# Shared keys of two heads in seven block products, and adaLN products moved and partly kept in float32

## The chip, the cores and the metric

The kernel runs on one core of a Trainium2 chip. The metric is the device time of one execution in microseconds (us); of several runs the median is taken. The core has TensorE (PE in the profile; its weight loads are PEld), VectorE (DVE), ScalarE (ACT), GpSimd (POOL) and SyncE (SP), which here only issues transfers.

## The reference

One step of a streaming encoder with two layers. 640 rows run through it: 512 of a prompt, and 8 sequences of 16 new rows. Layer 0 is a gated linear recurrence, layer 1 is stick-breaking attention over one shared set of keys and values. Width 2048, 16 heads of 128, all in float32.

```python
def ada_mod(c, w, b):
    m = jax.nn.silu(c) @ w + b          # c: 9 rows; w: 2048 x 6144
    shift, scale, gate = jnp.split(m, 3, axis=-1)
...
def shared_kv(x, g_kv, w_kv):
    k, v = jnp.split(rms_norm(x, g_kv) @ w_kv, 2, axis=-1)
...
for l in range(DEPTH):
    shift, scale, gate = ada_mod(c, w_ada[l], b_ada[l])
    hn = rms_norm(x, g_pre[l]) * (1.0 + scale) + shift
    # layer 0: out = recurrent_mixer(hn, ...)
    # layer 1: k_new, v_new = shared_kv(x, g_kv, w_kv); out = stick_breaking_mixer(hn, ...)
    x = x + gate * rms_norm(out, g_post[l])
```

The keys are 640 x 2048 by 2048 x 2048, and so are the values. adaLN has 9 rows of conditioning, so its products are thin.

## The kernel before

**Split products.** Float32 precision comes from two parts. A matrix is split into a high part, rounded by ScalarE (line 87), and a low part, the difference, made by VectorE (line 88). A product is then three on TensorE (lines 101 to 103): high by high, high by low, low by high. Weights arrive in raw tiles by SP's queue, are split into a ring of three buffers, wh and wl, and so run up to three blocks ahead of TensorE.

**Stages.** The opening and the recurrent layer (to 1017 us); the output product of layer 0 in two halves, each over eight pairs of k for four column chunks (to 1478); `mid`, which normalises and transposes rows, overlapped with the first of four value products; the keys (1545 to 1805); three more value products (to 1990); then query products and attention head by head; and the last output product. Engines run their queues in order. The order in each queue is made by a scheduler that takes instructions by priority and by when it expects their inputs, so a load or a split often stands far ahead of its place in the program text.

**The recurrent layer's pairs.** There, `pair_product` computes two 128-wide column blocks at once by seven block products in place of eight: k is paired (14 of 16 as 7 pairs), rows are halved (320 each), and four sums of the activations, S1 to S4, are made once by `combine`. Each `seven` is 21 products. The two k left over are done plainly (`plain`). The sums of the weights are made in transit, by accumulating transfers on GpSimd's queue (`pair_weights`, line 517). The weights' order of use is fixed by a generator, and `ahead` pulls it so that three splits stand ready.

**Keys and values (line 1013 on).** `values(n)` makes 512 columns of the values: 16 k x 5 row blocks x 3 products of 512 columns. `keys(h)` makes one head's keys plainly: 16 k x 2 halves x 3 products of 320 columns. The weights of a head come in two loads; GpSimd multiplies them by the norm's gain g_kv (line 1037), then they are split (lines 1039, 1040).

**adaLN (line 179 on).** A block is 512 columns of w_ada. `ada` does it in four groups; a group is two loads of 512 KB, each split into three bf16 parts (two ScalarE and two VectorE operations of 1024 columns, lines 185 and 186), then 12 bf16 products on 32-wide column tiles of TensorE, four at a time (line 198). A generator yields after each group, and other loops advance it. Layer 0's gates (4 blocks) run within the first half of the output product; layer 1's shifts, scales and gates (12 blocks) within the keys and the last value products.

Of the kernel before, what the change touches and what calls it, by code (L numbers as in the profile page):

```python
# [19 lines left out]
P = 128  # L20
D = 2048
# [27 lines left out]
class Trunk:  # L49
# [32 lines left out]
    def hilo(self, raw, width):  # L82

        nc, n = self.nc, raw.shape[1]
        hi = self.wp.tile([P, self.WW], F32R, tag="wh", name="wh", bufs=self.WB)
        lo = self.wp.tile([P, self.WW], F32R, tag="wl", name="wl", bufs=self.WB)
        nc.scalar.activation(hi[:, :n], raw, AF.Copy)  # L87
        nc.vector.tensor_tensor(lo[:, :n], raw, hi[:, :n].bitcast(F32), ALU.subtract)  # L88
        v = "p (a n) -> p a n"
        return hi[:, :n].rearrange(v, n=width), lo[:, :n].rearrange(v, n=width)  # L90

    def wraw(self, src, width):
        n = src.shape[1] * width
        raw = self.wp.tile([P, self.WW], F32, tag="wr", name="wr", bufs=self.RB)
        v = raw[:, :n].rearrange("p (a n) -> p a n", n=width)
        self.nc.sync.dma_start(v, src)
        return v
# [80 lines left out]
    def ada_split(self, src):  # L178

        nc = self.nc  # L180
        raw = self.adap.tile([P, 2, 512], F32, tag="wa", name="wa", bufs=self.abufs[0])
        nc.sync.dma_start(raw, src)
        parts = [self.adap.tile([P, 2, 512], BF16, tag=f"wa{i}", name=f"wa{i}", bufs=self.abufs[1]) for i in range(3)]
        for i in range(2):
            nc.scalar.activation(parts[i], raw, AF.Copy)  # L185
            nc.vector.tensor_tensor(parts[2] if i else raw, raw, parts[i], ALU.subtract)  # L186
        return parts

    def ada(self, w):


        nc = self.nc
        ps = self.bank("psa")
        for g in range(4):
            ws = [self.ada_split(w[:, k : k + 2, :]) for k in (4 * g, 4 * g + 2)]
            for i in range(3):
                for j in range(4):
                    nc.tensor.matmul(ps[32 * j : 32 * j + 32, :], self.c3[:, 4 * g + j, :], ws[j // 2][i][:, j % 2, :],  # L198
                                     start=g + i == 0, stop=g == 3 and i == 2)
            yield  # L200
        m = self.more.tile([P, 512], F32, tag="mod", name="msb", bufs=2)
        nc.scalar.activation(m, ps, AF.Copy)
        yield m

    def ada_cols(self, w, dst):

        for m in self.ada(w):
            if m is None:
                yield
# [45 lines left out]
    def ada_gate(self, l, c):  # L255

        nc, I = self.nc, self.I
        for m in self.ada(I["w_ada1"][12 * l + c]):
            if m is None:
                yield  # L260
# [12 lines left out]
    def ada_gates(self, l):  # L273
        for c in range(4):
            yield from self.ada_gate(l, c)

    def ada_rest(self):

        for part, dst in ((0, self.sh1), (1, self.gs1)):
            for c in range(4):  # L280
                dsts = [self.ada_dst(1, part, k, dst) for k in range(4 * c, 4 * c + 4)]
                yield from self.ada_cols(self.I["w_ada1"][4 + 4 * part + c], dsts)
        yield from self.ada_gates(1)
# [62 lines left out]
    def start(self, rp):  # L346
# [19 lines left out]
        for k in range(KD):  # L366
# [55 lines left out]
            elif k < 2 * NP:  # L422
                self.combine(rp, slot, even, tmp)
# [10 lines left out]
    def combine(self, rp, slot, even, odd):  # L434
# [3 lines left out]
        t = [rp.tile([P, HALF], F32, tag=f"s{i}", name=f"s{i}", bufs=1) for i in range(4)]  # L438
# [4 lines left out]
        n = slot[:, :, HALF * X11 : HALF * X11 + HALF]  # L443
        nc.scalar.activation(n, n.bitcast(F32), AF.Copy, scale=-1.0)
        for i, v in zip((S2, S3, S4, S1), (t[1], t[2], t[3], t[0])):
# [80 lines left out]
    def urgent(self, raw, width):  # L526
        with self.tc.high_priority(200):
            return self.hilo(raw, width)
# [35 lines left out]

    def ahead(self, held=0):
# [7 lines left out]
    def seven(self, ps, i, first):  # L573

        hi, lo = self.weights()
        c = slice(HALF * i, HALF * i + HALF)
        for n, x in enumerate(self.pairs):
            last = self.mm3(ps, hi[:, n, :], lo[:, n, :], x[:, 0, c], x[:, 1, c], first and n == 0, n == NP - 1, skip_group_check=True)
        return last

    def keep(self, ps, tag="keep", bufs=2):
        t = self.ep.tile([P, HALF], F32, tag=tag, name=tag, bufs=bufs)
# [211 lines left out]
    def recurrent(self, ep):  # L794

        self.ep = ep
        begun = self.opening()
# [14 lines left out]
    def out_product(self, src, w, chunks, evac, fill=iter(()), kept=(), urgent=False):  # L812
# [32 lines left out]
        for c, (toks, n) in enumerate(chunks):  # L845
# [10 lines left out]
            for k in range(0, early, 2):  # L856
# [7 lines left out]
                if c > 0:  # L864
# [39 lines left out]
    def rows(self, bp, x):  # L904

        ahead = None
        for t in range(TT):
            xs = [bp.tile([P, 512], F32, tag="xx", name="xx", bufs=8) for _ in range(4)]
            for n, v in enumerate(xs):
                self.nc.sync.dma_start(v, x[P * t : P * t + P, 512 * n : 512 * n + 512])  # L910
# [14 lines left out]
    def recurrent_out(self):  # L925
# [3 lines left out]
        with self.pool("oacc") as op:  # L929
# [5 lines left out]
            self.abufs = self.AB  # L935
            with self.pool("ada") as self.adap:
                rest = self.ada_gates(0)
                for _ in self.out_product([self.yd[0:D, :]], w[:, :, 0:KD, :], [(range(TT), n) for n in range(4)], keep, rest, urgent=True):
                    pass
            with self.pool("mid") as bp:  # L940
# [8 lines left out]

                chunks = [(x, n) for x in ((0, 1, 2), (3, 4)) for n in range(4)]  # L950
                for _ in self.out_product([self.yd[D:, :]], w[:, :, KD:, :], chunks, add):
# [61 lines left out]
    def shared_kv(self, bp, fill):  # L1013
# [3 lines left out]
        self.banks = [1, 2, 3, 4, 5, 0]  # L1017

        def tiles():
            return (self.wp.tile([P, self.WW], F32R, tag=n, name=n, bufs=self.WB) for n in ("wh", "wl"))  # L1020

        def load(n, k):

            raw = self.wraw(I["w_v"][n, :, k : k + 2, :], 512)
            hi, lo = tiles()
            for kk in range(2):
                s = slice(512 * kk, 512 * kk + 512)
                g = self.gkv[:, k + kk : k + kk + 1]
                nc.scalar.activation(hi[:, s], raw[:, kk, :], AF.Copy, scale=g)
                nc.vector.scalar_tensor_tensor(lo[:, s], raw[:, kk, :], g, hi[:, s].bitcast(F32),  # L1030
                                               op0=ALU.mult, op1=ALU.subtract)
            return hi, lo

        def load_k(h, k):

            raw = self.wraw(I["w_k"][h, :, k : k + 8, :], P)
            nc.gpsimd.tensor_tensor(raw, raw, self.gkv[:, k : k + 8].unsqueeze(2).broadcast_to([P, 8, P]), ALU.mult)
            hi, lo = (x.rearrange("p (k n) -> p k n", n=P) for x in tiles())
            nc.scalar.activation(hi, raw, AF.Copy)
            nc.vector.tensor_tensor(lo, raw, hi.bitcast(F32), ALU.subtract)  # L1040
            return hi, lo

        def values(n):
            ps = [self.acc("acck") for _ in range(TT)]

            def mm(k, t, hi, lo):
                s = slice(512 * (k % 2), 512 * (k % 2) + 512)
                ts = slice(P * t, P * t + P)
                mh, ml = self.hT[k]
                self.mm3(ps[t], mh[:, ts], ml[:, ts], hi[:, s], lo[:, s], k == 0, k == KD - 1)  # L1050

            def out(t):
                ev = bp.tile([P, 512], F32, tag="kve", name="kve", bufs=8)
# [5 lines left out]
            for toks in [(0, 1, 2), (3, 4)] if n == 0 else [range(TT)]:  # L1059
                for k in range(0, early, 2):  # L1060
                    w = load(n, k)
                    for kk in (k, k + 1):
                        for t in toks:
                            mm(kk, t, *w)
                    if n > 0:
                        next(fill, 0)
# [3 lines left out]
            tail = [load(n, k) for k in range(early, KD, 2)]  # L1070
            for t in range(TT):
                for k in range(early, KD):
                    mm(k, t, *tail[(k - early) // 2])
# [4 lines left out]
        def keys(h):  # L1078
            ps = [self.acc("acck")[:, :HALF] for _ in range(2)]
            for kc in (0, 8):  # L1080
                hi, lo = load_k(h, kc)
                for k in range(8):
                    mh, ml = self.hT[kc + k]
                    for j in range(2):
                        s = slice(HALF * j, HALF * j + HALF)
                        self.mm3(ps[j], hi[:, k, :], lo[:, k, :], mh[:, s], ml[:, s], kc + k == 0, kc + k == KD - 1)
                next(fill, 0)
            ev = bp.tile([P, T], F32, tag="ke", name="ke", bufs=3)
            for j in range(2):
                nc.scalar.activation(ev[:, HALF * j : HALF * j + HALF], ps[j], AF.Copy)  # L1090
            nc.gpsimd.dma_start(O["kT"][P * h : P * h + P, :], ev)

        values(0)
        for h in range(NHEAD):
            keys(h)
        for n in range(1, 4):
            values(n)
        for _ in fill:
            pass
# [329 lines left out]
    AB = (3, 4)  # L1429
    AD = (4, 4)  # L1430

    def run(self, upto="E"):
        tc, nc, I, O = self.tc, self.nc, self.I, self.O
        from contextlib import ExitStack
        with ExitStack() as ctx:
# [13 lines left out]
            self.WB, self.WW = 3, WQ  # L1449
            with self.pool("A") as self.ap, self.pool("w7") as self.wp:  # L1450
# [11 lines left out]
            self.WB, self.RB, self.WW = 3, 4, 1024  # L1462
# [6 lines left out]
            self.abufs = self.AD  # L1469
            with self.pool("ada") as self.adap:  # L1470
                with self.pool("kv") as bp:
                    self.shared_kv(bp, self.ada_rest())
# [7 lines left out]
def lay_in(a):  # L1480
# [21 lines left out]
    def features(rows):  # L1502
# [23 lines left out]
        "w_k": blocks(a["w_kv"][:, :D], P),  # L1526
# [32 lines left out]
```

## Time and profile before

| | us |
|---|---|
| median of 3 runs | 2883.09 (2879.89 to 2885.07) |
| profiled execution | 2886.43 |
| its span | 2884.3 |
| TensorE busy | 2826.2 |
| VectorE busy | 1965.5 |
| ScalarE busy | 1605.6 |
| GpSimd busy | 415.3 |

A row of the groups names the line, engine, operation, output and inputs by the program's tile names, the shape and the count; then the busy time, the mean duration in ns, and the engine's idle time before such instructions with what ended it. A row of the timeline has the start, the time taken and the instruction. A row of the windows has the stretch, its length, and busy time and count of each engine, then the granted TensorE clock, the share of the DMA engines and GB/s. A row of the waits names who waited for whom, the total, how often, and the longest. A float32 product stands in the trace as two records.

### The profile page before, as it was taken

To read this page: it belongs to the slowest core of one execution; us is meant where nothing else is said; L and a number is where in the kernel's file an instruction comes from. 1 tells how busy PE (TensorE), PEld (TensorE's weight loads), DVE (VectorE), ACT (ScalarE), POOL (GpSimd) and SP (SyncE) were. 2 spreads that over 40 slices of the span, in tenths; PEclk is the share of its full clock that TensorE was granted. 3 is DMA by queue.
4 is the path that set the end of the run, shared out by engine and by line. 5 is a ranking of instruction groups with operands and counts; after the bars stand their busy time and mean duration, and the time that the engine had idled before them with its cause. 6 is when DMAs were issued, how large, how long until landed. Compare 5 with 4: busy or idle time off the path is not lost.

```text
span 2884.3 us, 48196 instructions
## 1 busy us (share of the span) xinstructions
PE 2826.2 (98%) x18784; PEld 2514.8 (87%) x18784; DVE 1965.5 (68%) x2865; ACT 1605.6 (56%) x2464; POOL 415.3 (14%) x604
## 2 busy tenths in 40 slices
PE   6999999999999999999999999999999999998998
PEld 5799999999999987788778999778989889996787
DVE  7678767777777767543678777767766677666235
ACT  5476556655665566443566666753555555555223
POOL 0012211221122100001114221001000001101000
PEclk9999999999999999999999999999999999999999
DMA  9966766676667565654757666654556656567637
GB/s 328 331 146 156 165 160 156 157 165 160 154 158 165 121 243 184 186 181 131 251 188 239 212 215 208 214 173 145 175 177 195 197 184 194 172 209 273 174 110 226
DMA packets 249363, 546.33 MB, mean 189 GB/s; under 512 B 23000, under 2 KB 107096, under 8 KB 247984
## 3 DMA queue, kind: packets, MB, share of 16 engines
q1 hardware_dynamic: 221216, 446.92, 48.5%
q0 software_dynamic: 27920, 96.34, 15.7%
q8 instruction: 147, 2.41, 0.3%
q14 instruction: 80, 0.66, 0.1%
HBM read 501.15 MB, written 42.02 MB: 188 GB/s over the span
## 4 chain that ended last, share of the span: by engine, by line
PE 86%; DVE 3%; DMA 2%; ACT 1%; issue 1%; POOL 0%; SPq 0%; DVEq 0%; POOLq 0%; ACTq 0%
PE acc L101 6%; PE acc L103 6%; PE acc L102 6%; PE psh L101 5%; PE acck L101 5%; PE psh L103 5%; PE psh L102 5%; PE acck L102 5%; PE acck L103 5%; PE pa L101 3%; PE pa L103 3%; PE pa L102 3%; PE pc L103 2%; PE pc L101 2%; PE pc L102 2%; PE psa L198 2%
## 5 line engine op out<-in xcount | busy, mean ns | idle before, releaser
L88 DVE TENSOR_TENSOR wl<-wr,wh 128x1024 fp32r<-128x1024 f32 x216 | 269.7, 1251 | 306.0 <-ACT wh L87 305.6
L87 ACT ACTIVATE wh<-wr 128x1024 fp32r<-128x1024 f32 x216 | 228.1, 1057 | 408.2 <-PE acc L103 257.2
L101 PE MATMUL acc<-wh,yh 128*128 128x512 f32 x960 | 376.8, 393 | 3.1 <-ACT wh L87 3.0
L102 PE MATMUL acc<-wl,yh 128*128 128x512 f32 x960 | 375.3, 391 | 3.5 <-DVE wl L88 3.5
L103 PE MATMUL acc<-wh,yl 128*128 128x512 f32 x960 | 373.9, 390 | 1.3 <-DVE yl L837 1.3
L101 PE MATMUL psh<-nh,wh 128*128 128x320 f32 x1024 | 324.1, 317 | 0.0
L186 DVE TENSOR_TENSOR wa<-wa,wa 128x1024 bf16<-128x1024 f32 (+1 forms) x256 | 306.4, 1233 | 22.0 <-ACT wa L185 20.0
L103 PE MATMUL psh<-nh,wl 128*128 128x320 f32 x1024 | 319.0, 312 | 0.0
L102 PE MATMUL psh<-nl,wh 128*128 128x320 f32 x1024 | 317.6, 310 | 0.0
L185 ACT ACTIVATE wa<-wa 128x1024 bf16<-128x1024 f32 x256 | 263.1, 1052 | 61.6 <-DVE wa L186 42.7
L101 PEld LDWEIGHTS acc<-wh,yh 128*128 128x128 f32 x960 | 180.2, 188 | 50.6 <-issue 8.5
L102 PEld LDWEIGHTS acc<-wl,yh 128*128 128x128 f32 x960 | 180.6, 188 | 42.9 <-DVE wl L88 6.2
L103 PEld LDWEIGHTS acc<-wh,yl 128*128 128x128 f32 x960 | 180.6, 188 | 39.2 <-DVE yl L837 1.7
L101 PEld LDWEIGHTS psh<-nh,wh 128*128 128x128 f32 x1024 | 192.4, 188 | 19.3 <-DVE ql L1183 12.6
L103 PE MATMUL pa<-xs,wl 128*128 128x320 f32 x630 | 194.9, 309 | 0.5 <-DVE wl L88 0.5
L102 PE MATMUL pa<-xs,wh 128*128 128x320 f32 x630 | 194.8, 309 | 0.0
L101 PE MATMUL pa<-xs,wh 128*128 128x320 f32 x630 | 194.8, 309 | 0.0
L103 PEld LDWEIGHTS psh<-nh,wl 128*128 128x128 f32 x1024 | 192.5, 188 | 0.5 <-DVE wl L88 0.2
L102 PEld LDWEIGHTS psh<-nl,wh 128*128 128x128 f32 x1024 | 192.4, 188 | 0.1
L101 PE MATMUL acck<-nh,wh 128*128 128x320 f32 x512 | 161.6, 316 | 0.0
L103 PE MATMUL acck<-nh,wl 128*128 128x320 f32 x512 | 158.3, 309 | 0.0
L102 PE MATMUL acck<-nl,wh 128*128 128x320 f32 x512 | 158.2, 309 | 0.0
(357 smaller groups left out, 7213.6 us busy)
## 6 DMA issues: line engine op xcount, KB each, us to landing
wa<-w_ada_dram SPq DMA_DIRECT2D x192, 512.0 KB, 4.6
wr<-w_out_a_dram SPq DMA_DIRECT2D x96, 512.0 KB, 4.0
sum<-w_in_a_dram POOLq DMA_DIRECT2D x90, 448.0 KB, 5.6
wr<-w_in_b_dram SPq DMA_DIRECT2D x64, 512.0 KB, 5.5
ck<-cache_k_dram SPq DMA_DIRECT2D x64, 512.0 KB, 6.8
cv<-cache_v_dram SPq DMA_DIRECT2D x64, 512.0 KB, 5.4
wr<-w_out_b_dram SPq DMA_DIRECT2D x56, 512.0 KB, 3.8
raw<-w_in_a_dram SPq DMA_DIRECT2D x60, 448.0 KB, 4.2
```

Source lines behind the costliest of these rows:

```text
L87: nc.scalar.activation(hi[:, :n], raw, AF.Copy)
L88: nc.vector.tensor_tensor(lo[:, :n], raw, hi[:, :n].bitcast(F32), ALU.subtract)
L101: mm(out, sh, mh, start=start, stop=False, **kw)
L102: mm(out, sh, ml, start=False, stop=False, **kw)
L103: return mm(out, sl, mh, start=False, stop=stop, **kw)
L185: nc.scalar.activation(parts[i], raw, AF.Copy)
L186: nc.vector.tensor_tensor(parts[2] if i else raw, raw, parts[i], ALU.subtract)
L198: nc.tensor.matmul(ps[32 * j : 32 * j + 32, :], self.c3[:, 4 * g + j, :], ws[j // 2][i][:, j % 2, :], start=g + i == 0, stop=g == 3 and i ...
```

## The change

- The keys are done two heads at a time with the recurrent layer's `pair_product`. The four sums of the activations are made in the second value product, which now comes before the keys; X11, X12 and X22 are read from the activations as they lie. Where the recurrent layer negates X11, here the weights that meet it are negated as they are split.
- The keys' weights come as quarters. The chip multiplies them by g_kv in pieces of 128 columns (ScalarE or VectorE) and sums them on VectorE (`key_weights`). VectorE evacuates the four results of a pair.
- `ada` yields between a group's loads and splits and its products, so that these come with the next advance. A block can be done `whole`: float32 weights by float32 conditioning, 4 products a group, no split. Five of 16 blocks are whole.
- The blocks move: seven in the output product's first half, four in its second half, five in the last two value products; none in the keys.
- The raw tiles of weights have four names, each with one buffer, used in turn. Rows of the residual are loaded 1024 columns at a time.

```diff
-    def hilo(self, raw, width):
+    def hilo(self, raw, width, negative=False):
...
+        if negative:
+            nc.scalar.activation(hi[:, :n], raw, AF.Copy, scale=-1.0)
+            nc.vector.scalar_tensor_tensor(lo[:, :n], raw, -1.0, hi[:, :n].bitcast(F32), op0=ALU.mult, op1=ALU.subtract)
...
-    def ada(self, w):
+    def ada(self, w, whole):
...
         for g in range(4):
-            ws = [self.ada_split(w[:, k : k + 2, :]) for k in (4 * g, 4 * g + 2)]
-            for i in range(3):
+            ws = []
+            for k in range(4 * g, 4 * g + 4, n):
+                src = w[:, k : k + n, :]
+                if whole:
+                    parts = [self.adap.tile([P, n, 512], F32, tag=tag, name="wa", bufs=bufs)]
+                    nc.sync.dma_start(parts[0], src)
+                else:
+                    parts = self.ada_split(src)
+                ws += [[x[:, i, :] for x in parts] for i in range(n)]
+            yield
+            n_parts = len(ws[0])
+            for i in range(n_parts):
                 for j in range(4):
-                    nc.tensor.matmul(ps[32 * j : 32 * j + 32, :], self.c3[:, 4 * g + j, :], ws[j // 2][i][:, j % 2, :],
-                                     start=g + i == 0, stop=g == 3 and i == 2)
-            yield
+                    nc.tensor.matmul(ps[32 * j : 32 * j + 32, :], (self.c1 if whole else self.c3)[:, 4 * g + j, :], ws[j][i],
+                                     start=g + i == 0, stop=g == 3 and i == n_parts - 1)
...
+    def key_weights(self, sp):
...
+        def scale(tag, ks):
+            for j, k in enumerate(ks):
+                v, g = q[tag][:, P * j : P * j + P], self.gkv[:, k : k + 1]
+                if tag == "raw":
+                    V.tensor_scalar(v, v, g, None, op0=ALU.mult)
+                else:
+                    nc.scalar.activation(v, v, AF.Copy, scale=g)
+        def first(total):
+            scale("sum1", even)
+            scale("raw", even)
+            q["t"] = tile(total)
+            V.tensor_tensor(q["t"], q["sum1"], q["raw"], ALU.add)
...
+            yield split("t")
+            x = split("raw", True)
+            load("raw", w0, 3)
+            scale("rest", odd)
+            yield x
+            x = split("rest")
+            add("t", "rest")
+            add("rest", "sum1")
+            if w1 is not None:
+                load("sum1", w1, 1)
+            scale("rv", list(PLAIN) * 2)
+            yield x
+            yield self.urgent(q["rv"][:, :WV], P)
+            x = split("t")
+            scale("raw", odd)
+            add("t", "raw")
+            yield x
+            x = split("raw")
+            if w1 is not None:
+                load("raw", w1, 0)
+            yield x
...
+            x = split("t")
+            if w1 is not None:
+                first(("sum0", "total")[h % 2])
+            yield x
...
     def recurrent_out(self):
-                rest = self.ada_gates(0)
+                rest = chain(self.ada_shift(0, 0, True), *(self.ada_gate(0, c) for c in range(4)), *(self.ada_shift(0, c) for c in (1, 2)))
+                rate = lambda c, k: 1 if c else k % 4 // 2
...
+                self.adap, self.atags = bp, (("xx", 4, 2), ("nt", 3, 2), ("wa1", 2, 2), ("wa2", 2, 2))
+                rest = chain(self.ada_shift(0, 3), *(self.ada_shift(1, c, c == 2) for c in range(3)))
+                rate = lambda c, k: k % (4 if c < 4 else 8) == 2 if c else 0
...
     def shared_kv(self, bp):
         values(0)
-        for h in range(NHEAD):
-            keys(h)
-        for n in range(1, 4):
-            values(n)
+        with self.pool("sums") as sp:
...
+            def step(k):
+                if k < 2 * NP:
+                    slot = sp.tile([P, 2, 4 * HALF], F32R, tag="ks", name="ks", bufs=NP)
+                    t = [bp.tile([P, 512], F32, tag="kve", name="kt", bufs=5)[:, :HALF] for _ in range(4)]
+                    self.combine(t, slot, value(k), value(k + 1), (1, 2, 3, 0))
+                    sums.append(slot)
+                if k > 8:
+                    self.ready += [x for x in [next(self.planned)] if x]
...
+            self.planned = chain(self.key_weights(sp), (wide(2, k) for k in (0, 2, 4)))
+            values(1, step=step)
+            for q in range(NHEAD // 2):
...
+                self.pair_product(evac)
+        with self.pool("ada") as self.adap:
+            self.atags = [("wa", 6, 2)] + [(f"wa{i}", 4, 2) for i in range(3)]
+            fill = chain(self.ada_shift(1, 3), *(self.ada_gate(1, c, c > 0) for c in range(4)))
+            first, self.ready = self.ready, []
+            values(2, first, lambda k: [next(fill, 0) for _ in range(1 + (k > 6))])
+            values(3, (), lambda k: [next(fill, 0) for _ in range(1 + (k < 4))])
```

217 lines of the change are left out of this document (126 added, 91 removed).

## Prediction

> **What bounds the kernel now.** I read the page first (busy shares and the chain that ended last), then the chain of waits for TensorE, then its timeline in the stage that the change rewrites, and last the groups by shape for prices.
>
> ```profile
> span 2884.3 us, 48196 instructions
> PE 2826.2 (98%) x18784; PEld 2514.8 (87%) x18784; DVE 1965.5 (68%) x2865; ACT 1605.6 (56%) x2464; POOL 415.3 (14%) x604
> PE 86%; DVE 3%; DMA 2%; ACT 1%; issue 1%; POOL 0%; SPq 0%; DVEq 0%; POOLq 0%; ACTq 0%
> PE psn L327 <- DVE ssum L324: 17.9, 1, 17.9
> PE pss L228 <- DMA wa<-w_ada_dram: 5.3, 6, 2.3
> PE acc L102 <- DVE wl L88: 3.5, 6, 0.8
> 1018.00:1072.00 54.00, 52.67 (x232) 42.88 (x231) 43.21 (x54) 34.53 (x45) 5.42 (x8) 1.00 0.74 256
> 1478.00:1544.00 66.00, 64.30 (x313) 51.15 (x312) 56.67 (x87) 50.16 (x87) 11.77 (x12) 1.00 0.67 235
> 1545.00:1805.00 260.00, 260.00 (x1963) 238.65 (x1962) 199.43 (x187) 173.28 (x196) 72.91 (x47) 1.00 0.66 211
> ```
>
> TensorE carries the span: 98% busy, 86% of the chain. Its two longest waits lie in the opening, before any line that the change rewrites; the longest elsewhere is 3.5 us over six waits. In the keys' stage (1545 to 1805; the columns are PE, PEld, DVE, ACT, POOL busy, clock, DMA share, GB/s) it is busy for all 260 us. So a removed product is time won, a removed split is only relief, and a stall that appears anywhere in these stages is time lost.
>
> How much a product is worth is read from starts, not from durations:
>
> ```profile
> 1600.52 0.31 PE L103 MATMUL acck<-nh,wl 128*128 128x320 f32 x1
> 1600.76 0.83 PE L198 MATMUL psa<-wa,c 128*32 128x512 bf16 x12
> 1601.52 0.41 PE L101 MATMUL acck<-nh,wh 128*128 128x320 f32 x1
> 1601.77 0.31 PE L102 MATMUL acck<-nl,wh 128*128 128x320 f32 x1
> ...
> 1602.07 0.31 PE L101 MATMUL acck<-nh,wh 128*128 128x320 f32 x1
> ...
> 1608.52 0.31 PE L103 MATMUL acck<-nh,wl 128*128 128x320 f32 x1
> L101 PE MATMUL acck<-nh,wh 128*128 128x320 f32 x512 | 161.6, 316 | 0.0
> ```
>
> From 1602.07 to 1608.52 lie 44 products: 6.45 / 44 = 0.1466 us each, though one lasts 0.31. The group row's mean of 316 ns counts overlapped time twice. [...]
>
> **The change, part by part.**
>
> Keys. Before: 16 heads x 16 k x 2 halves x 3 = 1,536 products. After, per pair of heads: seven blocks x 7 k-pairs x 3 = 147, plus 2 plain k x 4 quarters x 3 = 24, so 171, and 8 pairs make 1,368. Gone are 168, worth 168 x 0.1466 = **-24.6 us**. (By the row's mean it would be -53; that is a rival below.) The products have the same shape, and the recurrent layer already runs such pairs; there the one thing that costs time is a bank that waits for its copy:
>
> ```profile
> 161.09 0.31 PE L101 MATMUL pd<-xs,wh 128*128 128x320 f32 x1
> 161.36 0.41 PE L101 MATMUL pa<-xv,wh 128*128 128x320 f32 x1
> 161.62 0.31 PE L102 MATMUL pa<-xv,wh 128*128 128x320 f32 x1
> ```
>
> 161.09 to 161.62 is 0.53 for two products that are worth 0.29: 0.24 a pair, 8 pairs: **+1.9**.
>
> adaLN. All 64 groups stay; 44 remain three bf16 parts, 20 (five blocks) become float32 products. A split group costs 1600.52 to 1601.77 less two products: 1.25 - 0.29 = 0.96. The float32 group of four is priced by the cached scores, of the same shape:
>
> ```profile
> 2034.51 0.31 PE L103 MATMUL psh<-nh,wl 128*128 128x320 f32 x1
> 2034.74 1.06 PE L1290 MATMUL zc<-ck,qs 128*32 128x512 f32 x8
> 2035.74 0.98 PE L1276 MATMUL pa<-ident,e 128*128 128x128 f32 x7
> ...
> 2037.65 0.42 PE L101 MATMUL psh<-nh,wh 128*128 128x320 f32 x1
> 2037.90 0.31 PE L102 MATMUL psh<-nl,wh 128*128 128x320 f32 x1
> ```
>
> 0.23 - 0.147 before it, 1.00 itself, 0.25 - 0.147 after it: 1.19. So 20 x (1.19 - 0.96) = **+4.6**. Putting the products a step behind their splits gains nothing on TensorE: no wait of psa stands in its list. It only lets the splits be late.
>
> Prices of what is moved to the other engines:
>
> ```profile
> L186 DVE TENSOR_TENSOR wa<-wa,wa 128x1024 bf16<-128x1024 f32 x128 | 154.1, 1234 | 3.5 <-ACT wa L185 1.8
> L88 DVE TENSOR_TENSOR wl<-raw,wh 128x896 fp32r<-128x896 f32 x60 | 65.4, 1089 | 20.3 <-ACT wh L87 17.8 <-PE psg L103 2.4
> L87 ACT ACTIVATE wh<-raw 128x896 fp32r<-128x896 f32 x60 | 56.9, 948 | 36.2 <-issue 30.6 <-PE pc L102 3.8 <-PE pa L102 1.1
> L337 DVE TENSOR_SCALAR diag<-ident,rs 128x128 f32<-128x128 f32 x5 | 1.1, 279 | 1.3 <-POOL rs L290 1.3
> L1185 ACT ACTIVATE qs<-psh 128x128 f32<-128x128 f32 x16 | 4.5, 278 | 1.3 <-DVE ql L1183 1.3
> L1029 ACT ACTIVATE wh<-wr,vec 128x512 fp32r<-128x512 f32 x80 | 55.5, 716 | 47.7 <-PE acck L103 45.1 <-PE acck L102 2.4 <-ACT wh L1029 0.2
> L1030 DVE SCALAR_TENSOR_TENSOR wl<-wr,vec,wh 128x512 fp32r<-128x512 f32 x80 | 60.3, 767 | 36.8 <-ACT wh L1029 36.6
> L724 DVE TENSOR_TENSOR zs<-pd,keep 128x320 f32<-128x320 f32 x15 | 7.4, 491 | 23.4 <-PE pd L103 23.4
> L1106 DVE TENSOR_TENSOR mod<-nh,nl 128x640 f32<-128x640 f32 x16 | 12.9, 819 | 0.1
> raw<-w_in_a_dram SPq DMA_DIRECT2D x60, 448.0 KB, 4.2
> ```
>
> Weights of a pair. VectorE gets 7 splits of 896 columns (1.09), 4 sums of that width (1.09), 14 scalings of 128 columns (0.279), 4 evacuations of 320 (0.49) and 2 splits of 256, taken at 0.49 too: 7.6 + 4.4 + 3.9 + 2.0 + 1.0 = 18.9 us. ScalarE gets 7 x 0.95, 18 scalings, and 6 operations of 320 or 256 columns, again at 0.49: with a scaling at 0.278 that is 14.6 us, with the 512-wide row's 0.716 as the upper end 22.5. A pair has 171 x 0.1466 = 25.1 us on TensorE, so both fit. Throughput is not the danger; the longest chain is. When X12 ends, the last block's weights are split, then head A's next sum is made and split, and it is due when S1 starts, 21 + 12 + 21 products or 7.9 us later. In that time: split 0.95 + 1.09, an evacuation 0.49, seven scalings 1.95, the sum 1.09, the high part 0.95, together 6.5. Cover 1.4 us. At the upper end of a 128-wide scaling (0.716) the chain is 9.6 and each pair would lose 1.7. The row of the very same shape, 0.279, is the nearest, so I take 0; a few tenths a pair stay in the range. The "raw" quarter that is scaled there is loaded once the sixth block's weights are split. That split follows the fifth's, which starts when X11 ends, 75 products or 11.0 us before X12 ends: split 2.04, scalings 1.95, sum 1.09, low part 1.09, so the load goes out 4.8 us before X12 ends and is first read 2.0 after. At its row's 4.2 it is in time; it may take 8.2 before the cover is used up. The GpSimd scaling goes away; TensorE's waits don't show it, so that is worth nothing.
>
> Sums of the activations. Each step of the second value product gives VectorE two adds (0.82), eight 320-wide operations (0.49) and a weight split (2 x 0.767): 7.1 us against 30 products. Their spacing:
>
> ```profile
> 1807.00 0.40 PE L101 MATMUL acck<-wh,nh 128*128 128x512 f32 x1
> ...
> 1812.90 0.39 PE L103 MATMUL acck<-wh,nl 128*128 128x512 f32 x1
> ```
>
> 26 products in 5.90 us, 0.227 each, 6.8 a step. Seven such steps overrun by about 2 us, which the stage before (1478 to 1544, VectorE busy 56.7 of 66, part of it adaLN splits that leave) can absorb: 0 to 2.
>
> adaLN in new places. In the second half of the output product a split group (4 x 1.23 = 4.9) meets two steps of 18 products (8.2 us): it fits, with two buffers for the last parts: 0 to 3. In the third value product two steps carry two split groups each: 9.9 + 1.5 = 11.4 us on VectorE against 6.8 + 2 x 0.96 = 8.7. The overrun of 5.4 must be taken from the lead that the splits have built up; the pool's memory is free only when S3 of the last pair is done, 33 products or 4.8 us before the stage, so the lead is small: 0 to 5. The last gate's row operations run past the last product, beside the first query's 28 us of products: 0 to 3. Of these four I take 3.5 in all, near the lower ends, because the present kernel runs 260 us with VectorE 77% busy and not one wait.
>
> The rest (wider loads of the residual rows, weights' raw tiles by name, the order of a negation in the opening) moves no work on TensorE: 0; uncovered, a microsecond.
>
> **Sum.** -24.6 + 1.9 + 4.6 + 3.5 = -14.6. The profiled execution took 2886.4 (span 2884.3 plus 2.1 around it), which becomes 2871.8; the median of the runs, 2883.1, lies 3.3 below it, so I forecast **2868.5**.
>
> **Rivals.**
>
> First, the gain is eaten by the weights' chain. Thirty-two scalings a pair, each of 128 columns, replace four wide GpSimd operations. By the rows a column costs 2.2 ns at 128 wide (0.279) and 1.2 at 896 (1.089), so small operations do pay a fixed part. [...] If the chain of 6.5 us, with the load's landing in it, comes to 9.4, each pair waits 1.5: +12, so 2880.5, no change that can be told. It decides from 7.9. Against it: the cover above. Chance 0.11.
>
> Second, slower: transfers in the last two value products. They take 20 groups x 1 MB, about 8 MB of weights and 2.6 MB of output, 31 MB in 480 products x 0.227 plus 22 us of adaLN groups, 131 us: 237 GB/s, with steps of two whole groups at 2.5 MB in 9.2 us, 272 GB/s. The stage at 1018 shows 256 GB/s at a DMA share of 0.74, so there should be room. If no more than 190 is granted, the stage lasts 163, +32: 2900.5. Below 213 GB/s it cancels the gain. Chance 0.06.
>
> Third, the mean duration is the price after all: -53 in place of -24.6, 2840. The spacing speaks against it. Chance 0.03.
>
> **Numbers.** My case: 0.80, from 2862 (no stalls, copies hidden) to 2877. The range, 2861 to 2884, takes in the first rival and leaves out the other two. A measurement can tell 0.2%, 5.8 us. Faster by more: 0.80 of my case less a little, plus the third, 0.81. Within: the first rival and the tail of mine, 0.12. Slower: 0.07.
>
> **What would show it.** Right: a keys' stage of about 203 us with 8 pairs at 25.1 and no psa in it; psa rows of 528 bf16 and 160 float32 records; still hardly any TensorE wait outside the opening. Wrong: TensorE waiting for wh or wl at each pair's first block (first rival), for wa or for weights' transfers in the last 130 us before the queries (second), or a float32 group far from 1.2 us.

## The result and the profile after

The changed kernel takes 2904.88 us (median of 4 runs, 2901.86 to 2907.28), the kernel before on the same chip 2883.44 (2879.89 to 2885.07): a ratio of 1.0075, 95% interval 1.0058 to 1.0093. It is slower by 0.75%, beyond the 0.2% that can be told from no change, where 14.6 us less were forecast. The profiled execution took 2902.89 us.

From the page of the changed kernel, the span, the busy line and the chain that ended last:

```profile
span 2901.2 us, 47975 instructions
PE 2819.2 (97%) x18536; PEld 2487.9 (86%) x18536; DVE 1995.2 (69%) x3074; ACT 1598.4 (55%) x2596; POOL 357.4 (12%) x588
PE 55%; DMA 4%; ACT 2%; DVE 2%; issue 1%; SPq 0%; POOL 0%; DVEq 0%; POOLq 0%; ACTq 0%
```

TensorE has less to do (2819.2 us busy, before 2826.2) and the span is 17 us longer: it idles. The chain says less here than it seems to: its shares add up to 64% of the span, where they were 93% before, and in the fastest kernel below TensorE has 30%. So the loss is looked for in the stages. The opening and recurrent layer (1018.0 us before, 1018.5 after) and all from the first query product on (894.4, 892.1) have hardly changed, so the loss lies between. The windows by stage, before (first half of the output product, second half, first value product, keys, three value products):

```profile
1018.00:1257.20 239.20, 237.87 (x1163) 183.12 (x1161) 145.46 (x146) 132.40 (x153) 15.36 (x28) 1.00 0.63 200
1257.20:1477.40 220.20, 218.65 (x962) 179.91 (x961) 115.26 (x135) 98.49 (x143) 28.44 (x25) 1.00 0.59 186
1477.40:1544.90 67.50, 65.80 (x322) 52.50 (x321) 58.17 (x88) 51.25 (x89) 13.27 (x12) 1.00 0.66 231
1544.90:1805.30 260.40, 260.40 (x1965) 238.99 (x1963) 199.53 (x187) 173.55 (x198) 73.01 (x47) 1.00 0.66 211
1805.30:1989.90 184.60, 184.60 (x943) 139.64 (x942) 140.73 (x187) 109.94 (x141) 14.27 (x27) 1.00 0.52 168
```

And after (first half, second half, two value products, keys, two value products):

```profile
1018.50:1273.70 255.20, 251.67 (x1282) 185.68 (x1280) 176.00 (x183) 157.42 (x181) 10.97 (x19) 1.00 0.67 222
1273.70:1529.80 256.10, 250.00 (x1205) 190.86 (x1201) 183.59 (x206) 150.24 (x200) 37.72 (x33) 0.98 0.74 239
1529.80:1655.40 125.60, 120.63 (x562) 97.80 (x561) 95.87 (x183) 74.88 (x150) 9.27 (x14) 1.00 0.41 130
1655.40:1866.10 210.70, 202.72 (x1370) 200.66 (x1369) 134.18 (x237) 107.16 (x234) 18.01 (x34) 1.00 0.36 113
1866.10:2009.10 143.00, 138.60 (x687) 95.64 (x686) 98.05 (x144) 69.10 (x91) 10.03 (x19) 0.98 0.66 225
```

The five sum to 971.9 before and 990.6 after: +18.7. Two columns matter. Length less TensorE's busy time is the idle time: none in the last two stages before; after, 8.0 in the keys, 6.1 in the second half, 4.4 in the last two value products. And the column after the counts of GpSimd, the granted clock, is 0.98 twice. After, no engine but TensorE is busy for more than 77% of a row, and the DMA share is 0.74 at most.

TensorE's waits from 1000 to 2000 us, before (the two longest of 4.3 us in all):

```profile
PE acc L102 <- DVE wl L88: 1.3, 2, 0.8
PE acc L103 <- DVE yl L837: 1.3, 1, 1.3
```

And after, of 27.3 us:

```profile
PE pa L106 <- ACT keep L680: 8.0, 7, 1.3
PE psc L228 <- ACT msb L218: 3.1, 1, 3.1
PE psg L278 <- ACT msb L218: 2.8, 1, 2.8
...
PE psa L215 <- DMA wa<-w_ada_dram: 2.2, 1, 2.2
PE acc L106 <- ACT wh L91: 2.2, 1, 2.2
PE acck L106 <- DVE keep L1212: 1.6, 1, 1.6
```

Most of them wait for ScalarE, which is busy for little over half the time. Three places show why.

**In each pair.** The timeline of ScalarE in the changed kernel, in the pair at 1750 (start, time taken, instruction):

```profile
1749.16 0.42 ACT L680 ACTIVATE keep<-pa 128x320 f32<-128x320 f32 x1
1752.22 1.28 ACT L600 ACTIVATE rest<-rest,vec 128x128 f32<-128x128 f32 x4 [2.65 <-DMA rest<-w_k_dram]
...
1756.31 0.93 ACT L91 ACTIVATE wh<-total 128x896 fp32r<-128x896 f32 x1
1757.15 0.41 ACT L680 ACTIVATE keep<-pa 128x320 f32<-128x320 f32 x1
```

and TensorE's at the same place:

```profile
1756.12 0.31 PE L108 MATMUL pd<-nh,wl 128*128 128x320 f32 x1
1757.61 0.41 PE L106 MATMUL pa<-nh,wh 128*128 128x320 f32 x1 [1.19 <-ACT keep L680]
```

The odd quarter `rest` stands at the head of ScalarE's queue before it has landed; ScalarE idles 2.65 us, and all that is queued behind, at the end the copy of S3's bank, comes later. TensorE starts its next product 1.49 after the start of the last, where 0.15 is the spacing: 1.3 us lost.

**In the second half of the output product.** ScalarE:

```profile
1297.63 1.28 ACT L1067 ACT_TABLE_LOAD   x1
1308.29 1.06 ACT L190 ACTIVATE wa<-wa 128x1024 bf16<-128x1024 f32 x1 [9.37 <-DMA wa<-w_ada_dram]
1309.25 1.04 ACT L91 ACTIVATE wh<-wr 128x1024 fp32r<-128x1024 f32 x1
```

Here the weights' split (wh) is queued behind an adaLN split whose transfer is late. The transfers issued from 1290 to 1312 (count, size, median us from issue to landing):

```profile
wr<-w_out_a_dram SPq DMA_DIRECT2D x3, 512.0 KB, 13.7
wa<-w_ada_dram SPq DMA_DIRECT2D x2, 512.0 KB, 17.7
gm<-grow POOLq DMA_DIRECT2D x7, 128.0 KB, 14.4
```

Over the whole kernel the same transfers of w_ada take a median of 5.1 us. The seven broadcasts of the gate rows (gm) run beside them; from 1255 to 1288 and from 1312 to 1340, without such rows, the medians are 4.4 and 4.6 for wa, 3.8 and 3.6 for wr. No run takes the broadcasts away, so that they make the loads late isn't shown.

**Behind the adaLN blocks.** TensorE at 1485, where the small product psc reads the copy msb of the block just finished:

```profile
1485.07 0.39 PE L107 MATMUL acc<-wl,yh 128*128 128x512 f32 x1
1488.59 1.75 PE L228 MATMUL psc<-sel,msb 128*128 128x16 f32 x8 [3.13 <-ACT msb L218]
1490.18 0.77 PE L108 MATMUL acc<-wh,yl 128*128 128x512 f32 x1
1490.75 0.63 PE L106 MATMUL acc<-wh,yh 128*128 128x512 f32 x1
...
1495.02 0.63 PE L107 MATMUL acc<-wl,yh 128*128 128x512 f32 x1
...
1495.98 0.40 PE L107 MATMUL acc<-wl,yh 128*128 128x512 f32 x1
```

The wait isn't all. For some microseconds after it a product takes 0.63 instead of 0.39, and products start 0.43 apart instead of 0.23. The window 1488.50 to 1495.50 has the granted clock 0.52:

```profile
1488.50:1495.50 7.00, 6.91 (x21) 5.75 (x22) 4.27 (x9) 3.23 (x7) 0.00 (x0) 0.52 1.00 349
```

Three such stretches (3.4, 6.8 and 6.8 us, at 1311, 1489 and 1960) stand in these stages of the changed kernel, each after a wait of 2.2 to 3.1 us; in the kernel before there is none. At half speed 17.0 us cost 8.5, an estimate.

### The profile page after: what moved, and what is told of

It is laid out like the page before. It is cut to its first block, busy times and chain, and to the rows that moved or that the text cites. A ratio compares the mean times of both kernels' runs of the same rounds, so it can differ in the third digit from the quotient of the medians.

```text
span 2901.2 us, 47975 instructions
## 1 busy us (share of the span) xinstructions
PE 2819.2 (97%) x18536; PEld 2487.9 (86%) x18536; DVE 1995.2 (69%) x3074; ACT 1598.4 (55%) x2596; POOL 357.4 (12%) x588
## 4 chain that ended last, share of the span: by engine, by line
PE 55%; DMA 4%; ACT 2%; DVE 2%; issue 1%; SPq 0%; POOL 0%; DVEq 0%; POOLq 0%; ACTq 0%
PE acc L106 7%; PE acc L107 7%; PE acc L108 6%; PE psh L106 6%; PE psh L108 5%; PE psh L107 5%; PE acck L106 2%; PE acck L107 2%; PE acck L108 2%; PE psa L215 2%; PE pos L1450 1%; PE zc L1415 1%; DMA rest<-w_k_dram 1%; DMA wa<-w_ada_dram 1%; ACT wh L91 1%
## 5 line engine op out<-in xcount | busy, mean ns | idle before, releaser
L191 DVE TENSOR_TENSOR wa<-wa 128x1024 f32<-128x1024 f32 (+1 forms) x176 | 211.5, 1244 | 15.5 <-ACT wa L190 14.2
L190 ACT ACTIVATE wa<-wa 128x1024 bf16<-128x1024 f32 x176 | 178.1, 1048 | 35.8 <-DMA wa<-w_ada_dram 17.7
L91 ACT ACTIVATE wh<-sum 128x896 fp32r<-128x896 f32 x102 | 96.7, 948 | 128.0 <-PE pb L107 41.4
L526 POOL DMA_DIRECT2D sum<-w_in_a_dram x90 | 79.0, 881 | 494.6 <-DVE wl L92 210.2
L91 ACT ACTIVATE wh<-rv 128x256 fp32r<-128x256 f32 (+1 forms) x108 | 51.8, 480 | 147.5 <-PE pa L107 95.6
```

Of the source, the lines that this page charges most:

```text
L526: self.nc.gpsimd.dma_start(self.big[tag], self.quarter(w, i), accum_op=ALU.add)
```

## The experiments

My theory: the prices are right, and what was missed are waits in in-order queues and the half clock that comes with them. Its parts are the pairs, the second half, and the place of the products behind the blocks. The rival: adaLN's move, or the pairs' many small operations, cost throughput, and the waits only show where. Each run is compared with the kernel before on its own chip; by this the changed kernel is at +21.4 us, its interval 16.7 to 26.8, so differences between runs of a few microseconds are read from the traces, above all from the stages between the recurrent layer and the queries (990.6 us in the changed kernel). A trace shows one run, with the half clock that this run happened to have.

**Products in the same step as their splits** (the generator yields behind a group's products, as before):

```diff
-            yield
             n_parts = len(ws[0])
...
                                     start=g + i == 0, stop=g == 3 and i == n_parts - 1)
+            yield
```

> The changed kernel with one thing undone: a group's products stand right behind its splits again and the pause comes after them, so a full step lies between a block's last products and the small product that uses ScalarE's copy of them. Theory 1 (the order): in the changed kernel TensorE reaches that small product before ScalarE has made the copy, and waits 3.1 us at 1485 and 2.8 us at 1957; the granted clock is halved for 6.8 us after each. Undone, both waits and both stretches of half clock go: 8 to 13 us less than the changed kernel, about 2893. Rival (the places): it is where the adaLN blocks lie that costs, through late transfers and a full ScalarE; then undoing the order changes nothing, or products right behind their splits wait for them and it is 3 us or more slower.

Measured: 2900.40 us (2897.77 to 2905.32), ratio 1.0058 (1.0045 to 1.0071): +15.8, 5.6 less than the change, between the two expectations. The stages take 989.4. TensorE's waits of these stages, from 1000 to 2000 us:

```profile
PE psa L214 <- DMA wa<-w_ada_dram: 3.6, 1, 3.6
...
PE psg L278 <- ACT msb L218: 2.5, 1, 2.5
```

The wait of psc at 1485 is gone, that of psg is still 2.5, and the products wait longer for their transfers (3.6 us, in the change 2.2) and 1.9 for a split. Putting the products a step behind is thus useful for the transfers and harmful for the small product; undoing it trades one wait for the other.

**Plain keys** (after the second value product, head by head with the old loop and weights in blocks; adaLN's blocks as in the change):

```diff
-            self.planned = chain(self.key_weights(sp), (wide(2, k) for k in (0, 2, 4)))
-            values(1, step=step)
...
+        values(1)
+        for h in range(NHEAD):
+            ps = [self.acc("acck")[:, :HALF] for _ in range(2)]
...
+                        self.mm3(ps[j], hi[:, k, :], lo[:, k, :], mh[:, s], ml[:, s], kc + k == 0, kc + k == KD - 1)
```

> The changed kernel with the keys done head by head and plainly, 1,536 products in place of 1,368, the weights scaled by GpSimd, no sums of activations; all adaLN blocks stay in their new places. If the seven block products are worth their 24.6 us less the 9 us that TensorE waits for the copy of S3 in the pairs and some 2 us around the stage, this is 11 to 16 us slower than the changed kernel, about 2918, and what makes the changed kernel slow is adaLN. Rival: the sums and scalings cost what the products save; then it is within 4 us of the changed kernel or faster.

Measured: 2910.94 us (2909.81 to 2912.92), ratio 1.0092 (1.0079 to 1.0106): +26.3, which is 4.9 above the change, between the two expectations. Its windows of the keys and of the last two value products:

```profile
1659.00:1884.30 225.30, 225.30 (x1538) 225.30 (x1537) 55.09 (x34) 45.33 (x67) 62.36 (x45) 1.00 0.32 103
1884.30:2021.10 136.80, 134.99 (x688) 94.13 (x687) 88.47 (x135) 61.84 (x85) 10.10 (x20) 1.00 0.57 194
```

So the change without its keys is the slow part: adaLN's move, with the wider loads and the names of the raw tiles, which no run takes from it. The shared keys gain 225.3 - 210.7 = 14.6 us in their stage, of the 22.7 forecast (24.6 - 1.9), and 143.0 - 136.8 = 6.2 go again in the stage behind; 3.4 of these are the half clock at 1960, which this run doesn't have there.

**GpSimd scales the odd quarter** (one operation of 896 columns in place of seven on ScalarE):

```diff
         def scale(tag, ks):
+            if tag == "rest":
+                v = q[tag].rearrange("p (k n) -> p k n", n=P)
+                g = self.gkv[:, 1 : 2 * NP : 2].unsqueeze(2).broadcast_to([P, NP, P])
+                nc.gpsimd.tensor_tensor(v, v, g, ALU.mult)
+                return
```

> The changed kernel with one scaling moved: the seven small ScalarE operations that scale the quarter named rest become one GpSimd operation of 896 columns. Theory 2 (the blocked queue): in each pair ScalarE stands still 2.65 us at the first of these until the quarter's transfer lands, and the copy of S3, queued behind, comes 1.2 us late for TensorE. With the wait on GpSimd the copy comes in time: 7 to 9 us less than the changed kernel, and the wait of about 1.3 us in each pair falls to 0.3 or less. Rival (the load): ScalarE has too many small operations in the pair; eleven of eighteen remain, so the wait falls by less than half, under 4 us.

Measured: 2893.66 us (2892.20 to 2895.65), ratio 1.0029 (1.0017 to 1.0041): +9.0. The window of its keys:

```profile
1653.80:1856.10 202.30, 202.17 (x1369) 200.65 (x1369) 141.66 (x240) 94.41 (x185) 30.03 (x41) 1.00 0.37 117
```

The seven waits are gone and the stage has the forecast length, about 203. The cause in the pairs is shown: the work that waits for the transfer stands on an engine where nothing urgent is queued behind it. The scaling costs 1.70 there and throughput was never the matter. The stage gains 8.4 us; the stages together gain 6.2 in this trace, since the waits for wh at 1305 and of psg at 1947 have grown to 4.3 and 4.6.

**The second half begins with its whole block**, which needs no split on ScalarE while the gate rows are loaded:

```diff
-                rest = chain(self.ada_shift(0, 3), *(self.ada_shift(1, c, c == 2) for c in range(3)))
+                rest = chain(self.ada_shift(1, 2, True), self.ada_shift(0, 3), *(self.ada_shift(1, c) for c in range(2)))
```

> The changed kernel with the order of the four adaLN blocks in the second half of the output product changed: the one kept whole, which has nothing to split, comes first. Theory 3: at 1308 ScalarE stands still 9.4 us at an adaLN split whose transfer is late beside the gate rows' broadcast, the weights' split behind it comes late, and TensorE waits 3.8 us and then has half the clock for 3.4 us. Without a split there the weights pass: 4 to 6 us less than the changed kernel. Rival: the weights' own transfers are late by as much; then the wait at this place stays, and the time is the same within 2 us.

Measured: 2896.44 us (2894.51 to 2900.49), ratio 1.0043 (1.0030 to 1.0056): +11.8. The second half:

```profile
1273.60:1523.70 250.10, 245.70 (x1205) 187.33 (x1202) 182.61 (x206) 150.35 (x200) 39.89 (x33) 1.00 0.75 245
```

It is 6.0 us shorter at the full clock; the wait at 1307 and its half clock are gone. The loads beside the gate rows are still late, and ScalarE waits 5.25 us there for the weights themselves, but they come before TensorE needs them. Part of the gain is luck: the wait of psc at 1485 is still 2.3 us, and this time no half clock follows it, which is worth 3.4. The wait of psg at 1951 has grown from 2.8 to 5.3.

**The small product one advance later**, behind the first group of the next block (the same for `psg`):

```diff
+            if g == 0:
+                self.flush()
...
-        ps = self.bank("psc")
...
-        self.ada_put(ps, dst)
+        def put():
+            ps = self.bank("psc")
...
+            self.ada_put(ps, dst)
+
+        self.pending.append(put)
```

> The products of an adaLN block stay a step behind their splits, but the small product that follows a block (psc, psg) is issued one advance later, after the first group of the next block, so that the copy msb it reads has a step's time. Theory: the waits for msb (3.1 us near 1485, 2.8 near 1957) are a matter of order in TensorE's queue, and the half clock that follows each costs 3.4 us more; then both waits and both half-clock stretches (6.8 us each) vanish and the time falls by 10 to 16, to 2889 to 2895. Rival: ScalarE is late by itself there (its splits wait for transfers), so that TensorE waits as long at the next thing it needs from ScalarE; then it falls by less than 4, to 2901 or more. The wait for weights at 1307 and the seven pair waits of 1.3 must stand in either case.

Measured: 2897.76 us (2893.10 to 2899.98), ratio 1.0042 (1.0029 to 1.0055): +12.0, 9 less than the change, between the two expectations. Its waits from 1000 to 2000 us:

```profile
PE pa L106 <- ACT keep L702: 7.5, 7, 1.2
PE acc L107 <- DVE wl L92: 4.8, 2, 3.8
```

No small product waits any more, and the last two value products take 136.2 us. But near 1490 the rival is right: TensorE stops 3.8 us at the next weights, whose split is late as well, since ScalarE itself waits there 3.20 us for VectorE's `oacc` rows. Both theories hold, each at one of the two places.

**Starts of stages** (the first half's whole block is advanced from k = 8 on, not from 2; the value products begin with a whole block):

```diff
-                rate = lambda c, k: 1 if c else k % 4 // 2
+                rate = lambda c, k: 1 if c else k // 8
...
-            fill = chain(self.ada_shift(1, 3), *(self.ada_gate(1, c, c > 0) for c in range(4)))
+            fill = chain(self.ada_shift(1, 3, True), self.ada_gate(1, 0), *(self.ada_gate(1, c, c > 1) for c in range(1, 4)))
```

> Two places where TensorE waited for a block's first transfer: the whole block of the first half is advanced in the last eight k of its chunk instead of from k=2 on, and the two last value products begin with a whole block (the first gate block is split instead; still five whole blocks). Theory: both waits are a buffer that comes free, or a transfer that is issued, too late for the place where its product stands; then the wait of 2.2 us at 1047 and the one of 1.6 at 1869 (VectorE's evacuation behind a split that waits for its transfer) go, and the time falls by 3 to 5, to 2900 to 2902. Rival: the transfers are short of bandwidth there, so that the wait moves to the next group; then the time stays within 2 us of 2905.

Measured: 2901.55 us (2897.07 to 2908.14), ratio 1.0059 (1.0045 to 1.0073): +15.8. The waits at 1047 and 1869 are gone, but psg now waits 6.4 us, where it had waited 2.8, and the mean clock of the profiled run is 0.992, in the change 0.994. The gain of 5.6 against the change lies within the interval of the two; by the trace the stages take 991.7 us, no less than the changed kernel's 990.6. In time the rival can't be excluded.

**All four edits, and two of them** (GpSimd's scaling and the second half's whole block):

> Four edits together: GpSimd scales the odd quarter of a pair in one operation, the second half's whole block comes first, the small products come one advance later, the stages begin as in the run before this one. If the lost time was TensorE's waits in queues and the half clock behind them, and each edit removes its own: 2905 - 11.2 - 8.5 (the first two, as measured alone) - 10 to 16 - 3 to 5 = 2864 to 2872, which is below the kernel before by 12 to 20. If the waits replace each other (the same late engine is met at the next tile), the sum of the first two remains: 2885, no change.

> Only the two edits already measured alone, together: GpSimd scales the odd quarter, and the second half's whole block comes first. If they act in stages that do not touch each other, 2905 - 11.2 - 8.5 = 2885, the same as the kernel before. If removing one only lets the other's wait grow, 2892 or more.

Measured: four edits 2875.24 us (2871.53 to 2877.52), ratio 0.9966 (0.9954 to 0.9979): -10.5, faster than both kernels, though a little short of the 12 to 20 expected. Two edits 2891.04 (2884.45 to 2900.08), ratio 1.0023 (1.0010 to 1.0035): +5.3, where the two single gains, 12.4 and 9.6 of 21.4, would have left -0.6. That difference lies within the intervals of the three, and in the stages the gains of the traces add up: 6.2 and 4.7 alone, 10.7 together. So it isn't shown that these two replace each other. The windows of the four edits, stages as after:

```profile
1017.70:1269.10 251.40, 250.08 (x1284) 186.43 (x1282) 176.56 (x184) 158.65 (x182) 11.01 (x19) 1.00 0.67 226
1269.10:1516.00 246.90, 245.19 (x1201) 186.99 (x1200) 182.12 (x207) 149.51 (x200) 38.55 (x34) 1.00 0.76 248
1516.00:1640.80 124.80, 120.49 (x561) 97.73 (x560) 95.55 (x176) 72.19 (x142) 11.14 (x15) 1.00 0.42 130
1640.80:1843.30 202.50, 202.17 (x1369) 200.65 (x1369) 141.90 (x240) 94.53 (x185) 30.64 (x41) 1.00 0.38 118
1843.30:1980.10 136.80, 136.19 (x689) 94.20 (x687) 97.40 (x144) 68.71 (x91) 10.06 (x19) 1.00 0.66 234
```

The clock is full in every stage, and idle time is below 2 us except in the third row, which had it already in the change. The work is that of the change: as many instructions on TensorE and VectorE, and 56 scalings of ScalarE have become 8 on GpSimd. Otherwise only places in the queues differ. That excludes throughput as the cause of the loss.

**Without the late small product** (three edits), and **the first half advanced 31 times** in place of 28 (with four edits; `k // 6`), so that its last group isn't left for the second half:

> The four edits without the late small product: three edits. Theory: the waits for the copy msb (psc, psg) are a cause of their own, found again and longer wherever the other waits have gone; then the two waits of 2 to 6 us and their half clock are back, and the time is 9 to 16 above the kernel of four edits (above 2884, no better than the kernel before). Rival: they were a result of the other three waits; then it is within 3 us of the kernel of four edits.

> The four edits as before, and the output product's first half advances its adaLN blocks 31 times instead of 28. It has 28 groups, whose products come a step behind, so that 28 advances leave the last group's products to the start of the second half, where the trace shows them in pieces of 2, 4 and 8 (seven pieces, 3.9 us, where one group of 12 costs 0.96). Theory: what the kernel of four edits still loses against the forecast are groups that are cut; then the pieces go and the time falls by 2 to 3.5 against that kernel (2875.2, 10.5 below the kernel before). Rival: the pieces are where they are because the splits are late, and only move; then it stays within 1 us.

Measured: three edits 2891.29 us (2884.38 to 2894.59), ratio 1.0021 (1.0013 to 1.0029): +7.3, which is 18 above the four, more than the 9 to 16 expected. Its waits:

```profile
PE psg L278 <- ACT msb L218: 7.0, 1, 7.0
PE psc L228 <- ACT msb L218: 2.1, 2, 1.8
```

So the small product behind its block is a cause of its own, and the largest one left: put later, it gained 9.4 alone and gains 18 as the last of four. Its wait at psg is 2.8 in the change and grows to 4.6, 5.3, 6.4, 3.9 and 7.0 in the runs that take other waits away; with the 7.0 the mean clock of the profiled run is 0.994, with the four edits 0.996. With 31 advances: 2874.11 us (2871.25 to 2877.78), ratio 0.9966 (0.9953 to 0.9979): -9.9, no difference to the four edits. The pieces at 1270 are one group again, and eleven new pieces stand between 1075 and 1100:

```profile
1077.97 0.40 PE L215 MATMUL psa<-wa,c 128*32 128x512 bf16 x4
...
1085.98 0.39 PE L215 MATMUL psa<-wa,c 128*32 128x512 bf16 x2
```

The cut groups only moved, as the rival has it; a gain of 2 to 3.5 us could hardly be told by the time. What cuts them stays open.

## Why the prediction was wrong

The terms of its sum, for the stages between the recurrent layer and the queries. Waits and groups are worked out from starts in the traces: the distance across a run of adaLN instructions less the spacing of the products around it (75.16 us in all before, 96.04 in the change, 84.94 with four edits). The last row is what remains of the stages' lengths.

| term, us | forecast | the change | four edits |
|---|---|---|---|
| 168 products fewer | -24.6 | -24.6 | -24.6 |
| keys beyond 1,368 x 0.1466 | +1.9 | +10.1 | +1.9 |
| adaLN on TensorE | +4.6 | +20.9 | +9.8 |
| the rest: other waits, half clock | +3.5 | +12.3 | +3.4 |
| sum | -14.6 | +18.7 | -9.5 |

- **The products** were priced rightly, by starts and not by the mean duration. The keys' stage was forecast at about 203 and takes 202.3 and 202.5 wherever the scaling is off ScalarE; the third rival (the mean as price) is out. Plain keys without adaLN took 225.3, 1,536 x 0.1466 = 225.2.
- **The copies, 0.24 a pair**: a step that failed, 1.3 a pair in the change. ScalarE's load per pair was forecast at 14.6 us or more and is 107.16 / 8 = 13.4, so there was room, and the chain that the prediction followed held. But of the loads only "raw" was followed to its use; `rest` was not, and nobody asked what is queued behind its first scaling. It is issued at 1747.92 and lands 4.2 us later; ScalarE could have used it at 1749.6. The kernel before had the sign of it, in two of its recurrent layer's pairs:

```profile
PE pa L101 <- ACT keep L584: 2.0, 2, 1.2
```

The longer of the two is at 197. ScalarE had stood still 3.08 us there at an operation that waited for VectorE, with the copy queued behind it, and by the starts the pair lost 1.46. The 0.24 is the price of a pair whose copy comes in time.
- **The first rival** named the right stage and nearly the right size (1.5 a pair), but the wrong thing waited for: not weights late for their block, but a bank not yet copied. The fixed part of small operations that it rested on, an estimate from two rows, isn't the cause: ScalarE's scalings of 128 columns follow each other 0.30 apart (four in 1.28, one 0.39), where 0.28 was forecast, so that the cost was in the price already.
- **The float32 groups** were priced rightly: 1.20 measured, 1.19 forecast; the split group 0.96, as forecast. What adaLN cost beyond that are, in the change, 8.1 us of its waits, some 2.4 of half clock on its small products, and about 6 for groups cut in pieces and small products that stand alone; with the four edits it is 0.6 of waits and about 5. A piece of two costs 0.53 as against 0.16 for its share of a whole group. "All 64 groups stay" counted work, not where the scheduler would put its parts.
- **The failed step** that weighs most is the four stalls, "I take 3.5 in all, near the lower ends, because the present kernel runs 260 us with VectorE 77% busy and not one wait". That stage proves that the engine has the time, not that each item is there in its order. In its place the change has 19.3 us of TensorE's waits outside the pairs, 15.0 more than before, and 8.5 lost at half clock, which the prediction priced nowhere; even the upper end of its range of 0 to 13 would have been short. "It only lets the splits be late" overlooked that the product a step behind brings its copy and the small product a step nearer to each other.
- **The second rival** (transfers in the last two value products): no. They get 225 GB/s in the change and 234 with four edits. The stage was worked out at 131. With four edits it is 136.8, with 0.6 of idle time and 27 us of adaLN where 22 were counted: the small products were left out, and groups are cut. The 143.0 of the change have 4.4 of idle time and 3.4 lost at half clock besides.
- **What would show it** did: "hardly any TensorE wait outside the opening" is the sign that failed. None of the waits named for the wrong case was the largest one.

What remains between the four edits and the forecast, 5.1 us in the table, lies in the adaLN row. That the last row comes out at the 3.5 forecast is luck: most of it is idle time around the first value product (4.3 us in that stage, 1.7 before), not the four stalls. Which part of the change's half clock and waits belongs to which row of the table can't be told exactly, since they overlap.

## What to carry to other kernels

Where one engine is busy for 98% of the time, the room on the others, as a sum over a stage, says little: for each instruction that waits for a transfer or a late engine, list what is queued behind it and who needs that. A step put "behind" another changes the distance to everything that follows it as well. And edits that remove waits are to be tried together too: alone, each of four here left a kernel slower than the one before, together they made the faster one, and the late small product was worth 9 us alone and 18 beside the other three.

## What the runs showed of the hardware

A wait of TensorE can cost more than its length. In the changed kernel it waited 2.2, 3.1 and 2.8 us from 1308.1, 1485.5 and 1957.7 on, and the stretches of half clock, of 3.4, 6.8 and 6.8 us, began 3.2, 3.3 and 2.1 us after the start of these waits. With the small product put later (the fifth experiment), TensorE waited 3.8 us from 1492.3 on, and from 1496.8 on a product again takes 0.63 in place of 0.39. Not every wait had it: around the 2.2 us at 1048 the window 1047.50 to 1060.00 has the clock 1.00, and so has the row of the keys, with seven waits of at most 1.3.

The mean granted clock of the profiled run is 0.996 in the kernel before and in the two runs with four edits, where the longest wait between 1000 and 2000 us is 1.3 us. It is 0.992 to 0.996 in the change and the other eight experiments, where the longest is 2.7 to 7.0. From what length on a wait brings half clock, and what sets the length of a stretch, isn't shown.
